# Hybrid attention-retention layer, one core: attention's q and k produced by features instead of by tokens; which third of the projection the first stage computes

## The chip, the cores and the metric

One NeuronCore of a Trainium2 chip runs the whole layer, 256 tokens by 1,024 features, in one launch. The metric is device time in microseconds. The kernel before was timed three times: 421.24, 421.24 and 421.31 us, median 421.24. All arithmetic is float32, and most matrix products are made from float32 operands split into a rounded high part and a remainder ("hi" and "lo"), with three products per pair: high by high, high by low, low by high.

## The reference, cut to what matters

```python
def token_mixer(h, w_in, w_proj_moba, w_proj_ret, w_out):
    proj = h @ w_in              # 256 x 1024 @ 1024 x 6656
    mq, mk, mv, rq, rk, rv, rg, g_a, g_r = split(proj)   # 512,512,512,512,512,1024,1024,1024,1024
    mq = rotary_half(split_heads(mq, 8), pos)   # 8 heads of 64: x1*cos - x2*sin, x2*cos + x1*sin
    mk = rotary_half(split_heads(mk, 8), pos)   # x1, x2: first and second 32 features of a head
    y_a = moba_attention(mq, mk, split_heads(mv, 8))     # 256 tokens: one block, plain causal attention
    rq = retnet_rotate(split_heads(rq, 4), pos)          # 4 heads of 128, features in even/odd pairs
    rk = retnet_rotate(split_heads(rk, 4), pos) * 128 ** -0.5
    y_r = head_norm(retention(rq, rk, split_heads(rv, 4)))   # decayed q k^T v, then mean 0, variance 1 per head
    y_r = silu(rg) * y_r
    merged = sigmoid(g_a) * (y_a @ w_proj_moba) + sigmoid(g_r) * (y_r @ w_proj_ret)
    return merged @ w_out
# around it: h = x * (1 + sc1) + sh1 with sc, sh from silu(c) @ w_ada; two layer norms; a gated FFN of width 2816
```

## The kernel before, in words

**First stage (0 to 63 us of the profiled execution).** The modulation vectors come from rows of `w_ada` by vector sums ("ada" work); as each of the eight 128-feature slices of the modulated input `h` is ready, it is multiplied with 2,048 columns of `w_in` (and the first four slices with those of g_a): all eight PSUM banks `pa[0..7]` collect mq and mk (1,024 columns, banks 0 to 3), mv (512, banks 4 and 5) and the first half of rv (512, banks 6 and 7), for both token halves. So q, k, v and rv arrive with tokens on the partitions.

**Main stage.** Everything else is a list of weight *units* of 1 MB (128 x 2,048). A unit is two halves and is worked off in two *steps* on PE. The list starts: four `wrot` units (rq and rk, units 0 to 3), six `winB` units (second half of rv, both halves of rg), two `winGa`, four `winGr`, two `wpm`, four `wpr`, and so on. Every half is prepared ahead: ScalarE (ACT) rounds it into `whi`, VectorE (DVE) subtracts to get `wlo` (`prep_halves`, eight buffers of each). There are two shapes of unit. `merged` (lines 134 and 138) keeps the weights stationary and gives results by features: 16 matmuls of 512 columns and 16 of 256. `xstat` (lines 123 to 125) keeps the input stationary and gives results by tokens: 24 matmuls of 512 columns.

**Side work.** `mixers` (attention) and `retention` are Python generators. `run_sides` advances them three times per step, and what they issue lands in the queues of PE, DVE and ACT between the pieces of the main list; nothing reorders it later, so each engine executes exactly the written order. Attention before: `evac_A` adds the two partial sums of q and k into `qk`; `rope` rotates them by tokens on DVE (lines 1020 to 1024, one call per token half), `rot_T` transposes both on PE (16 transposes, line 1030) into `qkT`; `scores` (line 1084) multiplies q by k for four heads per call, with 64 rows per head, so that two heads share the array; `maxima` (line 1093) masks and takes row maxima on DVE; ACT takes exponentials (line 1119) with sums; DVE the reciprocals (line 1123); ACT scales (line 1115); PE transposes the probabilities (line 1130); `attend` (line 1106) multiplies with v.

Retention's rq and rk come from `wrot` units, by features, one feature of each pair in one tile and its partner in another; `copied` moves the main and the correction part out of PSUM (line 499), `rotate` (lines 1001 to 1009) adds them and rotates on DVE. Scores (line 1190) and values (lines 1178 to 1180) follow on PE; mean and variance per head come from `bn_stats` and `bn_aggr` on DVE (lines 1170, 1171).

**Queues.** SP issues the weight loads in list order, each when one of four `raw` buffers is free; POOL issues the loads of `decay`, `x` and the norm rows. The constant tables are loaded on SP after the second unit (`CONST_AT`). Some of the later `ada` rows are mixed into the same stream (`extra`): two vector sums of 1,024 columns (line 257) per unit of theirs, placed after the preparation of a main half.

Of the kernel before, what the change touches and what calls it, by code (L numbers as in the profile page):

```python
# [19 lines left out]
RROPE, RET_AT, TL = 2, 10, 4  # L20
# [4 lines left out]
ROT_AT, RV_AT, RG_AT, LN1_AT = 4, 12, 20, 48  # L25
# [43 lines left out]
def _body(nc, a, out, pe, act, dve, sp, cst, wts, big, tmp, ps, dram):  # L69
# [267 lines left out]
    qk = [slot(n, [128, 1024]) for n in ("2a", "2b")]  # L337
# [151 lines left out]
    S = {}  # L489
    ghh, ghl = (lambda k: hh[:, k]), (lambda k: hl[:, k])  # L490

    S["rot"] = [slot(f"R{n}", [128, 4, 256]) for n in range(2)]
    S["rotl"] = [slot(n, [128, 4, 256]) for n in ("7a", "7b")]

    def wstat_rot(n, w):

        def copied(half, p):
            for i, o in enumerate((S["rot"][n], S["rotl"][n])):
                act.activation(o[:, 2 * w + half], p[:, i * 256:(i + 1) * 256], AF.Copy)
# [6 lines left out]
    def rv_done(bk):  # L506
        for t in range(2):
            act.activation(S["rv"][t][:, 512:], bk[t], AF.Copy)

    xstat("winB", 0, ghh, ghl, 8, lazy(two_banks), rv_done)  # L510
    for cc in range(2):
        def rg_done(bk, cc=cc):
            if cc == 0:
                S["rg"] = [slot(n, [128, 1024]) for n in ("7a", "7b")]
            for t in range(2):
                o = S["rg"][t][:, cc * 512:(cc + 1) * 512]
                act.activation(o, bk[t], AF.Silu)
        xstat("winB", 2 + 2 * cc, ghh, ghl, 8, lazy(two_banks), rg_done)
# [477 lines left out]
    def rotate(n):  # L996

        x, tmp_ = S["rot"][n], slot("8a", [128, 4, 256])
        xv, tv = (t.rearrange("p (w a) t -> p w a t", a=2) for t in (x, tmp_))
# [3 lines left out]
        for i in range(2):
            dve.tensor_tensor(tv[:, :, i], xv[:, :, 1 - i], bc(consts["sinr"], 2), OP.mult)
        yield
        dve.tensor_tensor(x, x, bc(consts["cosr"], 4), OP.mult)
        yield
# [3 lines left out]
    def rope(x, cos, sin):  # L1011

        n, w = cos.shape[-1], x.shape[-1]
        heads = w // n
        t2 = slot("8a", [128, w])
        hv = lambda t: t.rearrange("p (h n) -> p h n", n=n)
        bc = lambda v, m: v.unsqueeze(1).to_broadcast([128, heads, m])
        h2 = n // 2
        for i in range(2):
            dve.tensor_tensor(hv(t2)[:, :, i * h2:(i + 1) * h2],  # L1020
                              hv(x)[:, :, (1 - i) * h2:(2 - i) * h2],
                              bc(sin[:, i * h2:(i + 1) * h2], h2), OP.mult)
        dve.tensor_tensor(hv(x), hv(x), bc(cos, n), OP.mult)
        dve.tensor_tensor(x, x, t2, OP.add)

    def rot_T(roped, t, dst, which, b):

        p = bank(b)
        for i in range(4):
            pe.transpose(p[:, i * 128:(i + 1) * 128],  # L1030
# [453 lines left out]
```

## Time and profile before

| | |
|---|---|
| median of three runs | 421.24 us |
| profiled execution, its own time | 421.02 us |
| its span, first to last instruction | 419.3 us |
| PE busy | 413.1 us, 2,108 matmuls |
| DVE busy | 371.3 us |
| ACT busy | 246.7 us |
| granted TensorE clock | 0.997 |
| HBM traffic | 251 GB/s over the span |

The span is shorter than the time of its own run by 1.7 us, which lies before the first and after the last instruction. A matmul's listed duration overlaps that of the next one, so what a matmul costs in a stream is read from the distance between starts, not from its duration.

### The profile page before, as it was taken

How to read it: one execution, taken by the hardware profiler on the slowest of the kernel's cores; microseconds unless marked ns; L12 is line 12 of the kernel's file. 1: busy time of each engine (PE TensorE's matmuls, PEld its weight loads, DVE VectorE, ACT ScalarE, POOL GpSimd, SP SyncE). 2: the span in 40 equal slices, each digit the busy share in tenths (PEclk: the TensorE clock that was granted, in tenths of full speed). 3: DMA queues.
4: the chain of work that ended last, by engine and by line, in shares of the span. 5: the costliest groups of instructions: out<-in, count | busy, mean ns of one | idle time of the engine just before them, and what ended most of it. 6: DMA issues, size and time to landing. Idle time of an engine off the chain costs nothing.

```text
span 419.3 us, 5814 instructions
## 1 busy us (share of the span) xinstructions
PE 413.1 (99%) x2108; PEld 347.2 (83%) x2108; DVE 371.3 (89%) x605; ACT 246.7 (59%) x410; POOL 14.0 (3%) x26
## 2 busy tenths in 40 slices
PE   8999999999999999999999999999999999999995
PEld 4888888888878888888888898888888888888884
DVE  5979899969998889799787889899999998789996
ACT  4666568787855588535544886363563555455700
POOL 0000000100001000001000000100000000003200
PEclk9999999999999999999999999999999999999998
DMA  8998997685688778779672083995776877550002
GB/s 296 406 409 340 410 412 292 245 332 203 220 305 316 270 244 342 310 302 341 232 277 102 1 302 120 321 379 196 303 272 223 311 282 267 193 195 0 2 4 97
DMA packets 18540, 105.58 MB, mean 252 GB/s; under 512 B 2256, under 2 KB 3536, under 8 KB 7760
## 3 DMA queue, kind: packets, MB, share of 16 engines
q1 hardware_dynamic: 16992, 99.70, 63.0%
q0 software_dynamic: 1376, 4.99, 3.5%
q10 hardware_dynamic: 144, 0.52, 0.4%
q8 instruction: 16, 0.26, 0.3%
q14 instruction: 12, 0.10, 0.1%
HBM read 104.15 MB, written 1.06 MB: 251 GB/s over the span
## 4 chain that ended last, share of the span: by engine, by line
PE 98%; DVE 1%; issue 0%; DVEq 0%; ACT 0%; ACTq 0%
PE P L134 21%; PE P L123 14%; PE P L125 14%; PE P L124 14%; PE P L331 13%; PE P L138 11%; PE P L717 1%; PE P L720 1%; PE P L719 1%; PE P L1084 1%; PE P L243 1%; PE P L1190 1%; PE P L1106 1%; PE P L1130 1%; PE P L222 0%; PE P L661 0%
## 5 line engine op out<-in xcount | busy, mean ns | idle before, releaser
L1311 DVE TENSOR_TENSOR wlo<-raw,whi 128x1024 fp32r<-128x1024 f32 x118 | 141.6, 1219 | 11.6 <-ACT whi L1297 11.5
L1297 ACT ACTIVATE whi<-raw 128x1024 fp32r<-128x1024 f32 x118 | 121.7, 1056 | 33.9 <-PE P L125 10.8
L123 PE MATMUL P<-whi,AH 128*128 128x512 f32 x128 | 50.6, 395 | 0.0
L125 PE MATMUL P<-whi,AH 128*128 128x512 f32 x128 | 49.9, 390 | 0.0
L124 PE MATMUL P<-wlo,AH 128*128 128x512 f32 x128 | 49.8, 389 | 0.0
L134 PE MATMUL P<-AYa,whi 128*128 128x512 f32 x160 | 46.3, 391 | 0.0
L134 PE MATMUL P<-AYb,whi 128*128 128x512 f32 x160 | 43.0, 390 | 0.0
L331 PE MATMUL P<-whi,AH 128*128 128x512 f32 x160 | 41.6, 390 | 0.1
L257 DVE CUSTOM_DVE_ANT_0 junk<-raw,srow 128x1024 bf16<-128x1024 f32 x32 | 39.0, 1218 | 0.0
L331 PEld LDWEIGHTS P<-whi,AH 128*128 128x128 f32 x160 | 30.0, 188 | 7.1 <-ACT whi L314 0.9
L134 PEld LDWEIGHTS P<-AYb,whi 128*128 128x128 f32 x160 | 30.0, 188 | 6.6
L134 PEld LDWEIGHTS P<-AYa,whi 128*128 128x128 f32 x160 | 28.8, 189 | 4.7
L475 ACT ACTIVATE A<-P 128x256 f32<-128x256 f32 x40 | 15.0, 376 | 29.0 <-PE P L138 14.5
L314 ACT ACTIVATE whi<-raw 128x512 fp32r<-128x512 f32 (+1 forms) x26 | 20.8, 823 | 17.4 <-DMA raw<-in_b 16.1
L317 DVE TENSOR_TENSOR wlo<-raw,whi 128x512 fp32r<-128x512 f32 (+1 forms) x26 | 23.6, 935 | 6.0 <-ACT whi L314 5.5
L123 PEld LDWEIGHTS P<-whi,AH 128*128 128x128 f32 x128 | 24.0, 188 | 5.2 <-issue 0.3
L125 PEld LDWEIGHTS P<-whi,AH 128*128 128x128 f32 x128 | 24.0, 188 | 5.0
L124 PEld LDWEIGHTS P<-wlo,AH 128*128 128x128 f32 x128 | 24.0, 188 | 4.8
L138 PE MATMUL P<-AYb,wlo 128*128 128x256 f32 x160 | 25.7, 283 | 0.0
L138 PE MATMUL P<-AYa,wlo 128*128 128x256 f32 x160 | 25.6, 283 | 0.0
L138 PEld LDWEIGHTS P<-AYa,wlo 128*128 128x128 f32 x160 | 23.3, 190 | 1.6
L331 PE MATMUL P<-wlo,AH 128*128 128x512 f32 x80 | 23.2, 390 | 0.0
(308 smaller groups left out, 736.2 us busy)
## 6 DMA issues: line engine op xcount, KB each, us to landing
raw<-in_ada SPq DMA_DIRECT2D x16, 1024.0 KB, 4.9
raw<-in_wup SPq DMA_DIRECT2D x11, 1024.0 KB, 5.3
raw<-in_wgate SPq DMA_DIRECT2D x11, 1024.0 KB, 4.9
raw<-in_wdown SPq DMA_DIRECT2D x11, 1024.0 KB, 4.9
raw<-in_winB SPq DMA_DIRECT2D x6, 1024.0 KB, 5.4
raw<-in_m SPq DMA_DIRECT2D x4, 1024.0 KB, 8.1
raw<-in_b SPq DMA_DIRECT2D x4, 1024.0 KB, 7.3
raw<-in_wrot SPq DMA_DIRECT2D x4, 1024.0 KB, 7.9
```

Of the source, the lines that this page charges most:

```text
L123: pe.matmul(o, lh, rh, start=start, stop=False)
L124: pe.matmul(o, lh, rl, start=False, stop=False)
L125: pe.matmul(o, ll, rh, start=False, stop=stop)
L134: pe.matmul(banks()[half], t[0][:, k * 128:(k + 1) * 128], x2(k), start=k == 0, stop=half > 0 and k == 7)
L138: pe.matmul(banks()[half][:, :256], t[1][:, k * 128:(k + 1) * 128], x2(k)[:, 0], start=False, stop=half == 0 and k == 7)
L257: dve.tensor_tensor_reduce(out=nobody(j if own else None), in0=raw, in1=srow, scale=1.0, scalar=0.0, op0=OP.mult, op1=OP.add, accum_out=mo ...
L314: act.activation(hi[:, o], raw[:, o], AF.Copy)
L317: dve.tensor_tensor(lo[:, o], raw[:, o], f(hi[:, o]), OP.subtract)
L331: pe.matmul(pa[b0 + c // 512 * 2 + t], x[xi][:, j, t * 128:(t + 1) * 128], ws[k][:, c:c + 512], start=first and (xi, k) == (0, 0), stop=la ...
L475: act.activation(t, p[:, 256:], AF.Copy)
L1297: act.activation(hi, src, AF.Copy)
L1311: dve.tensor_tensor(lo, src, f(hi), OP.subtract)
```

## The change

- The first stage computes all of rv (1,024 columns, banks 0 to 3, kept in `S["rv"]`), mv as before, and the first half of rg (banks 6 and 7, through Silu on the way out of PSUM) instead of mq, mk, mv and half of rv.
- mq and mk become four more `wrot` units ahead of those of rq and rk: eight `wrot` units (steps 0 to 15), then two `winB` units (second half of rg). Tile `S["rot"][n]` for n = 0, 1 holds four heads of q and k: partitions 32e to 32e + 31 hold half of head e, the first and the second 32 features in separate slices. The total of units is the same.
- `rope` and `rot_T` are gone. `rotate` serves all four tiles, in two portions, put off to one and two steps after its second unit's last half.
- `scores` for four heads: for each head and query block two matmuls with 32 rows each, accumulated; the four heads sit on four row groups. It runs at the end of step 6 (heads 0 to 3) and of step 10 (heads 4 to 7), both times into banks 4, 7, 5, 6.
- The first two heads' probabilities are transposed one round later, into banks 4 and 7 (before: 5 and 6).
- Retention starts one step later. Its mean comes from the accumulating copies out of PSUM and its variance from eight Square activations on ACT instead of `bn_stats` and `bn_aggr` on DVE.
- cos and sin tables of both kinds are by features now: one extra load of 512 KB (`angles`) right after a smaller `tables` (180 KB; before 564 KB).
- The Sigmoid of `ga` is one activation per pair, put off by one or two steps.

```diff
-RROPE, RET_AT, TL = 2, 10, 4
+RET_AT, TL = 11, 4
-ROT_AT, RV_AT, RG_AT, LN1_AT = 4, 12, 20, 48
+SCORES_AT, RV_AT, RG_AT, LN1_AT = 6, 12, 20, 48
...
+        v = slot("8b", [128, 4, 256])
+        sp.dma_start(v, a["angles"])
+        for i, name in enumerate(ANGLES):
+            consts[name] = v[:, i]
...
-    S["rot"] = [slot(f"R{n}", [128, 4, 256]) for n in range(2)]
-    S["rotl"] = [slot(n, [128, 4, 256]) for n in ("7a", "7b")]
+    S["rot"] = [slot(n, [128, 4, 256]) for n in ("3a", "3b", "R0", "R1")]
+    S["rotl"] = [slot(n, [128, 4, 256]) for n in ("5", "15")] * 2
...
+            if w == half == 1:
+                turn = rotate(n)
+                put_off(1, lambda: next(turn))
+                put_off(2, lambda: next(turn))
         merged(a["wrot"][2 * n + w], lambda k: h1x2[:, :, k], copied)
-    for n in range(2):
+    for n in range(4):
         for w in range(2):
             wstat_rot(n, w)
...
     def rotate(n):
+        cos, sin = [consts[e + "mmrr"[n]] for e in ("cos", "sin")]
...
         dve.tensor_tensor(x, x, S["rotl"][n], OP.add)
+        for i in range(2):
+            dve.tensor_tensor(tv[:, :, i], xv[:, :, 1 - i], bc(sin, 2), OP.mult)
         yield
...
+        dve.tensor_tensor(x, x, bc(cos, 4), OP.mult)
         for i, op in enumerate((OP.subtract, OP.add)):
             dve.tensor_tensor(xv[:, :, i], xv[:, :, i], tv[:, :, i], op)
...
-        S["rv"] = [slot(n, [128, 1024]) for n in ("6a", "6b")]
+        S["rg"] = [slot(n, [128, 1024]) for n in ("7a", "7b")]
         for t in range(2):
-            act.activation(S["rv"][t][:, :512], pa[6 + t], AF.Copy)
+            act.activation(S["rg"][t][:, :512], pa[6 + t], AF.Silu)
...
-            S["sc"] = [bank(b) for b in ((4, 7, 5, 6), (2, 3, 4, 7))[h // 4]]
-            for w in range(2):
-                for qb, c in enumerate(blk):
-                    for e in range(2):
-                        s = slice(64 * e, 64 * e + 64)
-                        pe.matmul(S["sc"][2 * w + e][:, c], qkT[0][s, h // 2 + w, qb * 128:(qb + 1) * 128],
-                                  qkT[1][s, h // 2 + w, :128 + 128 * qb], start=True, stop=True)
+            S["sc"] = [bank(b) for b in (4, 7, 5, 6)]
+            x = S["rot"][h // 4]
+            for qb, c in enumerate(blk):
+                for i in range(2):
+                    for e in range(4):
+                        s = slice(32 * e, 32 * e + 32)
+                        pe.matmul(S["sc"][e][:, c], x[s, i, qb * 128:(qb + 1) * 128], x[s, 2 + i, :128 + 128 * qb],
+                                  start=i == 0, stop=i == 1)
...
-            for h in {4: (0, 1), 8: (2, 3, 4, 5), 10: (6, 7)}.get(i, ()):
+            for h in {5: (0, 1), 8: (2, 3, 4, 5), 10: (6, 7)}.get(i, ()):
                 sm, mx = st.pop(h)
-                p = bank(h - 2 if h in (2, 3) else 5 + h % 2)
+                p = bank((4, 7, 4, 7, 5, 6, 5, 6)[h])
...
-                    dve.bn_stats(stt[:, 2 * g + t % 2], yr[t % 2][:, g * 256:(g + 1) * 256])
-                    dve.bn_aggr(mv[:, 2 * g + t % 2], stt[:, 2 * g + t % 2:2 * g + t % 2 + 1])
+                    e = 2 * g + t % 2
+                    act.activation(square, yr[t % 2][:, g * 256:(g + 1) * 256], AF.Square, bias=mv[:, 1, e:e + 1],
+                                   accum_out=mv[:, 2, e:e + 1])
...
-        wrot=np.stack([ws(wi[:, RQ + 512 * w:][:, half_pairs(n)], 0, 2) for n in range(2) for w in range(2)]),
-        winB=np.stack(sum([xs(wi, RV + 512 * i) for i in range(1, 4)], [])),
+        wrot=np.stack([ws(wi[:, 512 * w:][:, half_heads(n)], 0, 2) for n in range(2) for w in range(2)] +
+                      [ws(wi[:, RQ + 512 * w:][:, half_pairs(n)], 0, 2) for n in range(2) for w in range(2)]),
+        winB=np.stack(xs(wi, RG + 512)),
```

How instructions stand now. The numbers behind names tell one buffer's uses apart and are not the same in both programs.

**ACT at the seam of the two stages.** `P4` to `P7` are the banks of mv and of rv (before) or rg (now); `whi` are the rounded weight halves of the main stage. Before:

```order
L1297 ACTIVATE whi_618<-raw_594 128x1024
L1045 ACTIVATE A4_624<-P4_130 128x512
L1045 ACTIVATE A4_624<-P5_131 128x512
L1048 ACTIVATE AYa_83<-P6_132 128x512
L1048 ACTIVATE AYb_84<-P7_133 128x512
L1297 ACTIVATE whi_634<-raw_594 128x1024
L1297 ACTIVATE whi_638<-raw_596 128x1024
L1297 ACTIVATE whi_644<-raw_596 128x1024
L499 ACTIVATE AR0_584<-P0_648 128x256
```

Now:

```order
L1260 ACTIVATE whi_620<-raw_596 128x1024
L1020 ACTIVATE A4_626<-P4_130 128x512
L1020 ACTIVATE A4_626<-P5_131 128x512
L1023 ACT_TABLE_LOAD
L1023 ACTIVATE A7a_629<-P6_132 128x512
L1023 ACTIVATE A7b_630<-P7_133 128x512
L1260 ACTIVATE whi_633<-raw_596 128x1024
L1260 ACTIVATE whi_637<-raw_598 128x1024
L1260 ACTIVATE whi_643<-raw_598 128x1024
L502 ACTIVATE AYa_83<-P0_647 128x256
```

The two copies of rv have become two Silu of rg, with a table load ahead of them, and the weight halves 5, 6 and 7 stand behind it.

**DVE in steps 0 to 6.** `A2a`, `A2b` are q and k by tokens, `AYa` the first tile of q and k by features, `A5` its correction part. Before:

```order
L1311 TENSOR_TENSOR wlo_616<-raw_590,whi_608 128x1024
L1311 TENSOR_TENSOR wlo_620<-raw_590,whi_614 128x1024
L1020 TENSOR_TENSOR A8a_629<-A2a_134,tables_592 128x16x32 x2
L1023 TENSOR_TENSOR A2a_134<-A2a_134,tables_592 128x1024
L1024 TENSOR_TENSOR A2a_134<-A2a_134,A8a_629 128x1024
L1311 TENSOR_TENSOR wlo_636<-raw_594,whi_618 128x1024
L1311 TENSOR_TENSOR wlo_640<-raw_594,whi_634 128x1024
L1311 TENSOR_TENSOR wlo_646<-raw_596,whi_638 128x1024
L1020 TENSOR_TENSOR A8a_669<-A2b_135,tables_592 128x16x32 x2
L1023 TENSOR_TENSOR A2b_135<-A2b_135,tables_592 128x1024
L1024 TENSOR_TENSOR A2b_135<-A2b_135,A8a_669 128x1024
L1311 TENSOR_TENSOR wlo_693<-raw_596,whi_644 128x1024
```

Now (the first row is half 6; `wlo_741` is half 10):

```order
L1274 TENSOR_TENSOR wlo_645<-raw_598,whi_637 128x1024
L1274 TENSOR_TENSOR wlo_687<-raw_598,whi_643 128x1024
L1274 TENSOR_TENSOR wlo_693<-raw_614,whi_685 128x1024
L1274 TENSOR_TENSOR wlo_735<-raw_614,whi_691 128x1024
L1274 TENSOR_TENSOR wlo_741<-raw_624,whi_733 128x1024
L1002 TENSOR_TENSOR AYa_83<-AYa_83,A5_586 128x1024
L1004 TENSOR_TENSOR A8a_743<-AYa_83,A8b_594 128x2x256 x2
L1006 TENSOR_TENSOR AYa_83<-AYa_83,A8b_594 128x1024
L1008 TENSOR_TENSOR AYa_83<-AYa_83,A8a_743 128x2x256 x2
L1274 TENSOR_TENSOR wlo_792<-raw_641,whi_739 128x1024
L1274 TENSOR_TENSOR wlo_798<-raw_641,whi_790 128x1024
```

The two rotations by tokens, each between weight halves early in the stage, are gone; one rotation by features stands behind half 10.

**DVE between the first and the second group of scores.** `mx` are row maxima of a head, `junk` rows are the `ada` sums. Before, behind the maxima of heads 2 and 3:

```order
L1001 TENSOR_TENSOR AR0_584<-AR0_584,A7a_586 128x1024
L1311 TENSOR_TENSOR wlo_924<-raw_743,whi_887 128x1024
L257 ISA junk_926,mod_82<-raw_695,srow_100 128x1024
L257 ISA mod_82 128x1
L1123 RECIPROCAL mx_914<-mx_914 128x2
L1004 TENSOR_TENSOR A8a_920<-AR0_584,tables_592 128x2x256 x2
L1311 TENSOR_TENSOR wlo_951<-raw_743,whi_922 128x1024
L257 ISA junk_955,mod_82<-raw_821,srow_100 128x1024
L257 ISA mod_82 128x1
L1123 RECIPROCAL mx_917<-mx_917 128x2
L1093 ISA A11_848,mx_998<-P2_986,tables_592 128x128
```

Now, from the same place:

```order
L1006 TENSOR_TENSOR AYb_84<-AYb_84,A8b_594 128x1024
L1008 TENSOR_TENSOR AYb_84<-AYb_84,A8a_888 128x2x256 x2
L1086 RECIPROCAL mx_914<-mx_914 128x2
L1274 TENSOR_TENSOR wlo_947<-raw_737,whi_876 128x1024
L261 ISA junk_951,mod_82<-raw_794,srow_100 128x1024
L261 ISA mod_82 128x1
L1274 TENSOR_TENSOR wlo_955<-raw_872,whi_945 128x1024
L261 ISA junk_957,mod_82<-raw_794,srow_100 128x1024
L261 ISA mod_82 128x1
L1086 RECIPROCAL mx_917<-mx_917 128x2
L1055 ISA A11_821,mx_1007<-P4_987,tables_592 128x128
```

Where a quarter of retention's rotation stood, which PE reads only at line 1190, stands now the second half of the rotation of `AYb`, the q and k of heads 4 to 7, which line 1046 (their scores) reads next. Its first half stands ahead of the maxima of heads 2 and 3, behind two weight halves and two `ada` sums that follow the first reciprocal. The maxima of head 4 in the last row read bank 4, which is also the bank of head 0's transposes.

More of the change, by code (lines that the diff above doesn't have):

```diff
@@ L335, in g_prod @@
         x_prod(f"g{j}", ks, j == 0, j == 3)
-    qk = [slot(n, [128, 1024]) for n in ("2a", "2b")]
+    S["rv"] = [slot(n, [128, 1024]) for n in ("2a", "2b")]
     ga = slot(12, [128, 4, 512])
@@ L499, in copied, with rg_done @@
                 act.activation(o[:, 2 * w + half], p[:, i * 256:(i + 1) * 256], AF.Copy)
+            if w == half == 1:
+                turn = rotate(n)
+                put_off(1, lambda: next(turn))
+                put_off(2, lambda: next(turn))
         merged(a["wrot"][2 * n + w], lambda k: h1x2[:, :, k], copied)
-    for n in range(2):
+    for n in range(4):
         for w in range(2):
             wstat_rot(n, w)
-    def rv_done(bk):
+    def rg_done(bk):
         for t in range(2):
[L508 to L518, printed above, removed]
+            act.activation(S["rg"][t][:, 512:], bk[t], AF.Silu)
+    xstat("winB", 0, ghh, ghl, 8, lazy(two_banks), rg_done)
     for c in range(2):
@@ L1001, in rotate @@
         dve.tensor_tensor(x, x, S["rotl"][n], OP.add)
+        for i in range(2):
+            dve.tensor_tensor(tv[:, :, i], xv[:, :, 1 - i], bc(sin, 2), OP.mult)
         yield
[L1003 to L1007, printed above, removed]
+        dve.tensor_tensor(x, x, bc(cos, 4), OP.mult)
         for i, op in enumerate((OP.subtract, OP.add)):
             dve.tensor_tensor(xv[:, :, i], xv[:, :, i], tv[:, :, i], op)
[L1011 to L1030, printed above, removed]
-                         roped[:, which * 512 + i * 128:which * 512 + (i + 1) * 128], ident)
-        act.activation(dst[which][:, :, t * 128:(t + 1) * 128],
-                       p.rearrange("p (i t) -> p i t", i=4), AF.Copy)
+        yield
     def evac_A():
@@ L1107, in attend @@
                                   v[:, kb, 64 * u:64 * u + 64], pT[e][:, c], start=kb == 0, stop=kb == 1)
-            return lambda: split(yah[:, h // 2:h // 2 + 2], yal[:, h // 2:h // 2 + 2], p.rearrange("p (w t) -> p w t", w=2))
-        for i in range(HM + 5):
+            return lambda: split(S["yah"][:, h // 2:h // 2 + 2], S["yal"][:, h // 2:h // 2 + 2],
+                                 p.rearrange("p (w t) -> p w t", w=2))
+        for i in range(HM + 6):
             yield
@@ L1139, in mixers @@
                 maxima(i + i % 2)
-            if i == RROPE:
-                S["turn"] = [rotate(n) for n in range(2)]
-            if i >= RROPE and S["turn"] and next(S["turn"][0], 1) == 1:
-                S["turn"].pop(0)
             if i == RET_AT:
@@ L1150, in retention @@
     def retention():
-        rot, decay, sms = S["rot"], S["decay"], S["sms"]
+        rot, decay, sms = S["rot"][2:], S["decay"], S["sms"]
         while S["main"] < RV_AT:
@@ L1156, in retention @@
         rv = S["rv"]
-        yr = [slot(n, [128, 1024]) for n in ("8a", "8b")]
-        SCORES, VALUES = ((4, 7), (2, 3)), (5, 6, 4, 7)
-        stt = tmp.tile([128, 8, 6], F32, name="stt", bufs=1)
-        mv = tmp.tile([128, 8, 2], F32, name="mvr", bufs=1)
+        SCORES, VALUES = ((4, 7), (0, 1)), (5, 6, 4, 7)
+        mv = tmp.tile([128, 3, 8], F32, name="mvr", bufs=1)
+        square = decay[0][:, 0, :256]
         sd = tmp.tile([128, 8], F32, name="sdr", bufs=1)
@@ L1216, in retention @@
                 for t in range(2):
[L1217 to L1218 removed]
+                    dve.scalar_tensor_tensor(yr[t][:, c], yr[t][:, c], mv[:, 1, 2 * g + t:2 * g + t + 1], srg[t][:, c],
+                                             op0=OP.add, op1=OP.mult)
             yield
@@ L1225, in retention @@
             yield
-        for _ in range(11):
+        for _ in range(8):
             yield
@@ L1471 @@
     ins.update(_tables())
+    ins["angles"] = np.stack([ins.pop(n) for n in ANGLES], 1)
     ins["tables"] = np.concatenate([np.asarray(ins.pop(n), dtype=np.float32).reshape(128, -1) for n, _ in TABLES], 1)
```

55 lines of the change are left out of this document (22 added, 33 removed).

## The prediction

> **What bounds the kernel now.** I read the page's busy times and its chain first, then the windows by stage, then the timelines of PE, ACT and DVE between 62 and 102 us, where the change moves work.
>
> ```profile
> span 419.3 us, 5814 instructions
> PE 413.1 (99%) x2108; PEld 347.2 (83%) x2108; DVE 371.3 (89%) x605; ACT 246.7 (59%) x410; POOL 14.0 (3%) x26
> PE 98%; DVE 1%; issue 0%; DVEq 0%; ACT 0%; ACTq 0%
> ```
>
> The third line is the chain that ended last: 98% of the span lies on PE. So a microsecond of PE work added or removed is a microsecond of time, and so is a microsecond in which PE waits. DVE is at 89%, so the second question is whether DVE can still deliver on time. The windows (time, then busy time of each engine) say where:
>
> ```profile
> 62.98:84.53 21.55, 21.55 (x130) 19.05 (x128) 21.14 (x21) 17.13 (x31) 1.27 (x2) 1.00 0.75 272
> 84.53:101.99 17.46, 17.46 (x102) 14.29 (x102) 13.69 (x42) 14.49 (x39) 0.00 (x0) 1.00 0.72 270
> 101.99:128.73 26.74, 26.74 (x167) 21.98 (x165) 25.04 (x44) 18.93 (x42) 0.00 (x0) 1.00 0.73 272
> 128.73:172.00 43.27, 43.27 (x194) 36.09 (x193) 39.52 (x68) 28.66 (x44) 1.06 (x2) 1.00 0.81 290
> ```
>
> PE has no gap in any of them. The third busy column is DVE: 21.1 of 21.6, 13.7 of 17.5, 25.0 of 26.7. From the start of the main stage to retention DVE has almost no room.
>
> **PE's own work.** PE's timeline (start, duration of the run, line, count; the distance between starts is the cost):
>
> ```profile
> 62.98 2.20 PE L134 MATMUL P<-AH,whi 128*128 128x512 f32 x9
> 66.94 3.82 PE L134 MATMUL P<-AH,whi 128*128 128x512 f32 x16
> 72.50 3.82 PE L134 MATMUL P<-AH,whi 128*128 128x512 f32 x16
> 79.69 1.03 PE L1030 MATMUL P<-ident,A2a 128*128 128x128 f32 x8
> 80.56 1.04 PE L1030 MATMUL P<-ident,A2b 128*128 128x128 f32 x8
> 81.35 2.30 PE L134 MATMUL P<-AH,whi 128*128 128x512 f32 x9
> 84.53 1.58 PE L1084 MATMUL P<-AYb,AYa 64*128 64x128 f32 x16
> 86.04 1.22 PE L138 MATMUL P<-AH,wlo 128*128 128x256 f32 x8
> 88.72 0.39 PE L123 MATMUL P<-whi,AH 128*128 128x512 f32 x1
> 96.88 0.82 PE L1130 MATMUL P<-ident,A 128*128 128x128 f32 x6
> 97.63 1.58 PE L1084 MATMUL P<-AYb,AYa 64*128 64x128 f32 x16
> 99.14 0.50 PE L123 MATMUL P<-whi,AH 128*128 128x512 f32 x1
> ```
>
> *Four units change shape.* A `merged` unit takes 72.50 - 66.94 = 5.56 us. Between 88.72 and 96.88 stand three `xstat` steps of 12 matmuls: 8.16 / 36 = 0.227 us each, 5.44 us a unit of 24. Four units cost 4 x 0.12 = +0.48 us.
>
> *Sixteen transposes go:* 81.35 - 79.69 = -1.66 us.
>
> *Scores.* One call takes 86.04 - 84.53 = 1.51 us (99.14 - 97.63 gives the same), for 16 matmul records on two row groups of 64. The new call has 32 records of the same widths on four row groups of 32, an arrangement that this trace does not show. If four run at once as two do now, the call stays at 1.51; if only two do, it is 3.02. I take 1.51, since the row is one of row groups that do run side by side, and keep 3.02 as the other end. The sum for the two calls is 0 to +3.0.
>
> In sentences of their own: the Trainium skill, "TensorE: Matmul & The Clock Gate", Part 3 on packing small matmuls, gives 3.07 times the speed for four row tiles of 32, not four times. By that a call would be an estimated 1.51 x 4 / 3.07 = 2.0 us; it speaks against the case of only two at a time, and this trace, with two groups only, can't show it.
>
> So without any new wait PE gains 1.66 - 0.48 = **1.2 us**. That is what the change is worth if DVE and ACT are never late.
>
> **When q and k are ready now.** Before, `rope` ran from the first step on, and PE's transposes came at 79.69 with time to spare. Now the rotation can start only when units 0 and 1 are through PE (62.98 + 2 x 5.56 = 74.1), and it stands behind half 10 in DVE's queue. When half 10 comes is set by ACT, whose timeline before is:
>
> ```profile
> 65.94 1.07 ACT L1045 ACTIVATE A<-P 128x512 f32<-128x512 f32 x2
> 66.90 0.60 ACT L1048 ACTIVATE AYa<-P 128x512 f32<-128x512 f32 x1
> 67.37 0.61 ACT L1048 ACTIVATE AYb<-P 128x512 f32<-128x512 f32 x1
> 67.85 2.97 ACT L1297 ACTIVATE whi<-raw 128x1024 fp32r<-128x1024 f32 x3
> 70.70 0.40 ACT L499 ACTIVATE AR<-P 128x256 f32<-128x256 f32 x1
> 71.75 2.06 ACT L1297 ACTIVATE whi<-raw 128x1024 fp32r<-128x1024 f32 x2
> 85.31 1.28 ACT L1119 ACT_TABLE_LOAD   x1
> 86.61 0.40 ACT L1119 ACTIVATE A<-A,mx 128x128 f32<-128x128 f32 x1
> 87.41 0.19 ACT L1119 ACTIVATION_READ_ACCUMULATOR A<-A,mx 128x1 f32 x1
> ```
>
> Three halves take 70.70 - 67.85 = 2.85 us, 0.95 each, and four copies of a step pair 71.75 - 70.70 = 1.05. The table load for Silu is new at this place: 1.28 us by the row of the one for Exp. The old order from 66.90, with the load: load to 68.2; two Silu as the two copies, 0.95, to 69.15; halves 5 to 7, to 72.0; copies of unit 0, to 73.05; halves 8 and 9, to 74.95; copies of unit 1, whose results are there since 74.1, to 76.0; half 10, whose last element is there at 77.1. ACT has no pause in this stretch.
>
> DVE, where the times of the operations come from the same operations before:
>
> ```profile
> 66.59 1.29 DVE L1020 TENSOR_TENSOR A8a<-A2a,tables 128x512 f32<-128x512 f32 x2
> 67.91 1.22 DVE L1023 TENSOR_TENSOR A2a<-A2a,tables 128x1024 f32<-128x1024 f32 x1
> 69.17 1.22 DVE L1024 TENSOR_TENSOR A2a<-A2a,A8a 128x1024 f32<-128x1024 f32 x1
> 70.31 3.49 DVE L1311 TENSOR_TENSOR wlo<-raw,whi 128x1024 fp32r<-128x1024 f32 x3
> 85.49 0.29 DVE L1093 CUSTOM_DVE_ANT_0 A<-P,tables 128x128 f32<-128x128 f32 x1 [0.78 <-PE P L1084]
> 86.05 0.28 DVE L1093 CUSTOM_DVE_ANT_0 A<-P,tables 128x128 f32<-128x128 f32 x1
> 86.61 0.08 DVE L1093 DVE_READ_ACCUMULATOR2_ANT mx<- 128x1 f32 x1
> 87.63 0.17 DVE L1123 RECIPROCAL mx<-mx 128x2 f32<-128x2 f32 x1 [0.94 <-ACT A L1119]
> 87.72 1.21 DVE L1311 TENSOR_TENSOR wlo<-raw,whi 128x1024 fp32r<-128x1024 f32 x1
> 88.84 1.22 DVE L257 CUSTOM_DVE_ANT_0 junk<-raw,srow 128x1024 bf16<-128x1024 f32 x1
> 89.98 0.09 DVE L257 DVE_READ_ACCUMULATOR2_ANT mod<- 128x1 f32 x1
> ```
>
> A pair of 512 takes 1.32 from start to start when the next operation needs it, a 1,024-wide one 1.26; one that needs nothing follows 1.14 after. A weight half or an `ada` sum takes 1.14, the maxima of a head 86.05 - 85.49 = 0.56. A rotation is two wide operations and two pairs: 1.26 + 1.32 + 1.26 + 1.2 = 5.0 us.
>
> *First scores.* Half 10's remainder 77.1 to 78.3, rotation to **83.3**. PE, without transposes, reaches the scores after 3 units and the stretch that took 84.53 - 81.35 = 3.18: 62.98 + 16.68 + 3.18 = **82.84**. PE waits about 0.4 us: scores from 83.2 to 84.75.
>
> *Second scores.* DVE goes on from 83.3: two halves (85.6), maxima of heads 0 and 1 (86.7), then the reciprocal, which waits for ACT's exponential of head 0. Head 0's maxima are there at 86.15, and the exponential of a head takes from 86.61 to 87.6, 1.0: 87.15. Then half, `ada`, half, `ada` (4.6: 91.8), the first half of the rotation of heads 4 to 7 (2.5: 94.3), the maxima of heads 2 and 3 (1.1: 95.4), the second half (2.5): **97.9**. PE from 84.75: rest of step 6 and step 7, 88.72 - 86.04 = 2.68; one unit, 5.56; step 10, 3.18: **96.2**. PE waits 1.7 us, less the quarter of the scores that needs only the first half of the tile (0.2): 1.5. The scores end at about 99.2.
>
> *First transposes.* PE does step 11 (2.68) and is at 101.9 at the transposes of heads 0 and 1, now in banks 4 and 7, which heads 4 and 5 have just filled. DVE empties them after half, `ada`, half, `ada` (4.6) and 0.56: 97.9 + 4.7 + 0.56 = **103.2**, and 103.75 for bank 7. PE waits 1.3 and 0.2 us. Before, these transposes used banks 5 and 6, long empty.
>
> Together PE waits 0.4 + 1.5 + 1.5 = **3.4 us**. All three waits lie on one chain of DVE work from 77.1 to 103.7 with one pause of 0.4. So the cost of the scores on PE hardly enters: a slower call takes the place of a wait.
>
> **After that.** Where DVE takes retention's scores, it had time before:
>
> ```profile
> 127.52 1.02 DVE L1193 TENSOR_TENSOR A<-P,A2a 128x384 f32<-128x384 f32 x2 [1.48 <-PE P L1190]
> ```
>
> It was there at 126.04 and waited 1.48 us for PE. Behind 104 us it has one rotation, one half and one `ada` sum more than before ahead of this place; adding the rows in the new order it is there at 132.0, 6.0 later. PE comes 2.4 us later by the sum below and has one step (12 x 0.227 = 2.7) more, 5.1 later. So DVE's pause shrinks to about 0.6, and no wait of PE arises. Weight halves are four or more ahead of PE at all three waits above, so none of them becomes a wait either. From 128.73 on, DVE loses `bn_stats` and `bn_aggr`, and ACT gets eight Squares with sums, some 0.6 us each by the exponential's rows: 28.7 + 5 of 43.3 us. Both are taken as free; if Squares stood in the way of a weight half, they would cost up to these 5 us, but the halves are ahead. The constant loads (692 against 564 KB, an estimated 0.5 us at the window's 272 GB/s) lie ahead of unit 2's weights on SP's queue; ACT rounds the second half of unit 2 at 67.85 before and at 69.15 now, and it is the Silu that it waits for. They cost 0.
>
> **The sum.** -1.66 + 0.48 + 0 (scores) + 3.4 = **+2.2 us**, and about 0.1 us for the stream that restarts after a wait (0.50 against 0.39 us in the rows at 99.14 and 88.72): +2.4 in round numbers. Against the profiled execution's own 421.02 us that is 423.4. This execution lies 0.22 us under the median, so I predict **423.6 us**.
>
> **Rivals.**
>
> *DVE keeps up.* Then only PE's work counts: 421.24 - 1.2 = 420.0 us, faster. The place is half 10. If it did not stand behind ACT's Silu and copies, the rotation could start at 75.1, when ACT has copied unit 1 out (74.1 + 1.05), and be done at 80.1, 3.2 us earlier, and the whole chain with it; nearly all of the waits would go. For it: a wait for several events may end earlier than I take it to. Against it: ACT's rows add up without a pause. It decides from 3 us of gain on; every us less than that leaves one us more of waiting: 1.5 us of gain gives 421.9, inside no change.
>
> *Only two row groups at a time.* Scores take 3.02. The first call then ends at 86.2, DVE's maxima start 0.9 us later than above, the second rotation ends at 98.8, the second call at 101.5; after step 11 PE is at 104.2, and bank 4 is ready by then. The transposes end 0.9 us later than in the forecast: 424.5 us.
>
> *A fourth wait, in retention.* DVE's pause at the decay products is only 0.6 us. If the chain between 104 and 132 us is 3 us longer, by exponentials that come late for the reciprocals between its halves, the products and with them the value matmuls come some 2 us late: 425.6 us. It decides from 0.6 us of delay on. Against it: this stretch has the same kinds of rows as before, in which DVE arrived early.
>
> **How the numbers follow.** Chances: waits as computed, within a microsecond, 0.50; two row groups 0.12; fourth wait 0.10; DVE partly early (between 420.4 and 422) 0.12; DVE keeps up 0.16. A measurement of this kernel can tell about 0.2% (0.84 us) from no change. Faster by more than that is the last case alone, 0.16; no change 0.13 with the edges of its neighbours; slower 0.71. The likeliest case by itself spans 422.6 to 424.6. The range takes in the slower cases and most of the partly early one: **420.3 to 425.6**.
>
> **What would show it.** In the new PE timeline: no line 1030, a gap ahead of the scores at line 1046 of about 0.4 and 1.5 us and one ahead of the first transposes at line 1094, all released by DVE; DVE nearly without a pause from half 10 to the maxima of head 4. Scores of 1.5 us show four row groups side by side, of 3 us two. No Silu load between the first stage's copies, or half 10 on DVE before 75 us, would make the first step wrong, and PE without gaps there the whole forecast.

## The result, and the profile after

The changed kernel takes **425.85 us** (median of 4 runs, 425.27 to 426.35) against 421.27 us for the kernel before beside it (4 runs): ratio 1.0108, 95% interval 1.0090 to 1.0125. It is slower, as forecast, but by 4.6 us where 2.4 were computed; 425.85 lies 0.25 us above the range. The profiled execution took 426.35 us, the longest of its four. All ratios here and below are of runs at a granted clock of 0.989 or more; a single run of 591.64 us at 0.657, of the kernel with blocks 8 and 15 below, is left out of them.

The page of the changed kernel (span; busy times and counts; the chain that ended last):

```profile
span 424.6 us, 5936 instructions
PE 413.3 (97%) x2156; PEld 347.1 (82%) x2156; DVE 370.6 (87%) x593; ACT 252.3 (59%) x441; POOL 14.0 (3%) x26
PE 87%; DVE 6%; ACT 3%; DMA 2%; issue 1%; DVEq 0%; ACTq 0%
```

PE is busy for 413.3 us, as before (413.1). The chain, 98% PE before, is now 87% PE: the rest passed to DVE, ACT and the transfers. So PE does no more work than before (a part of the 413.3 us is even pauses inside rows, see below); it waits. The view of waits, for PE (what it waited for, total, times, longest):

```profile
PE P L134 <- ACT A L502: 1.4, 1, 1.4
PE P L1046 <- DVE AYa L1008: 1.3, 1, 1.3
PE P L1094 <- DVE mx L1055: 1.2, 1, 1.2
PE P L1046 <- DVE AYb L1008: 1.1, 1, 1.1
```

None of the four is there before; together 5.0 us. PE's timeline puts them in place:

```profile
75.76 2.35 PE L134 MATMUL P<-AH,whi 128*128 128x512 f32 x9 [1.38 <-ACT A L502]
85.94 1.97 PE L1046 MATMUL P<-AYa 32*128 32x128 f32 x32 [1.33 <-DVE AYa L1008]
87.85 1.22 PE L138 MATMUL P<-AH,wlo 128*128 128x256 f32 x8
100.29 1.97 PE L1046 MATMUL P<-AYb 32*128 32x128 f32 x32 [1.06 <-DVE AYb L1008]
102.20 1.22 PE L138 MATMUL P<-AH,wlo 128*128 128x256 f32 x8
106.23 1.07 PE L1094 MATMUL P<-ident,A 128*128 128x128 f32 x6 [1.20 <-DVE mx L1055]
```

The last three stand where the prediction put its waits. The first, inside unit 2, is new: the next matmul of unit 2 needs a bank from which ACT has not yet copied unit 0. A scores call takes 87.85 - 85.94 = 1.91 us, which looks like a slower array, but is not; see the experiments.

Why is ACT late? Its rows in the changed kernel:

```profile
67.90 1.06 ACT L1260 ACTIVATE whi<-raw 128x1024 fp32r<-128x1024 f32 x1 [3.27 <-DMA raw<-in_wrot]
69.94 1.28 ACT L1023 ACT_TABLE_LOAD   x1
79.05 2.08 ACT L1260 ACTIVATE whi<-raw 128x1024 fp32r<-128x1024 f32 x2
```

and the same weight half (half 4, the first of unit 2) before:

```profile
64.98 1.06 ACT L1297 ACTIVATE whi<-raw 128x1024 fp32r<-128x1024 f32 x1 [1.91 <-PE P L134]
```

Before, ACT took half 4 at 64.98; now it takes it at 67.90, 2.9 us later, and waited for the **transfer** of the weights. The row of before names PE as what ended the wait, but the view of DMA issues shows that there too the transfer came last (KB, us from issue to landing, of unit 2's load; before, then after):

```profile
raw<-in_wrot SPq DMA_DIRECT2D x1, 1024.0 KB, 8.8
raw<-in_wrot SPq DMA_DIRECT2D x1, 1024.0 KB, 11.2
```

Issued at 56.04 us, the load landed at 64.84 before; issued at 56.60, it lands at 67.8 now. So 0.6 of the 2.9 us are a later issue (in this execution SP is already 0.6 us later at 48.3 us, ahead of every load that the change moved), and 2.4 us are a longer transfer. The table load (1.28) and everything behind it are as computed, only some 3 us later: half 10 is taken at 79.05, computed was 76.0.

What delays the transfer? The issues on SP and POOL, before:

```profile
53.79 0.42 SPq L163 DMA_DIRECT2D tables<-in_tables  x1
56.04 3.87 SPq L110 DMA_DIRECT2D raw<-in_wrot  x2
81.04 0.72 POOL L1072 DMA_DIRECT2D A2a<-in_decay  x1 [79.67 <-DVE wlo L1311]
```

and after:

```profile
53.49 0.72 POOL L1033 DMA_DIRECT2D AYa<-in_decay  x1 [52.11 <-ACT A7a L306]
58.21 0.54 POOL L1033 DMA_DIRECT2D AYb<-in_decay  x1 [4.00 <-ACT A7b L306]
54.83 0.47 SPq L189 DMA_DIRECT2D A8b<-in_angles  x1
56.60 18.28 SPq L110 DMA_DIRECT2D raw<-in_wrot  x5
```

The two loads of retention's decay table (384 KB each, from the tile's 128 x 2 x 384 float32) have moved from 81 to 53 and 58 us. Nobody wrote them there: they now go into tiles 6a and 6b instead of 2a and 2b, those tiles are free early, and POOL issues a load as soon as its tile is free. With the new `angles` load on SP, 1.25 MB stand in the stretch in which the weights of units 2 and 3 arrive. The windows of that stretch (the last three columns are clock, busy share of the transfer engines and GB/s), before:

```profile
66.00:68.00 2.00, 2.00 (x15) 1.82 (x14) 1.97 (x4) 2.00 (x6) 0.00 (x0) 1.00 0.88 340
```

and after:

```profile
66.00:68.00 2.00, 2.00 (x15) 1.82 (x15) 1.49 (x2) 0.10 (x1) 0.00 (x0) 1.00 1.03 426
```

Before, the transfers had room here and ACT (fourth busy column) was busy for all 2.00 us. After, they are full at 426 GB/s and ACT does 0.10 us of work.

DVE continues from there. Its rows after (half 10; start of the first rotation; end of the second; maxima of head 4; decay products):

```profile
80.22 1.22 DVE L1274 TENSOR_TENSOR wlo<-raw,whi 128x1024 fp32r<-128x1024 f32 x1 [0.62 <-ACT whi L1260]
81.36 1.22 DVE L1002 TENSOR_TENSOR AYa<-AYa,A 128x1024 f32<-128x1024 f32 x1
99.55 1.29 DVE L1008 TENSOR_TENSOR AYb<-AYb,A8a 128x512 f32<-128x512 f32 x2
105.46 0.27 DVE L1055 CUSTOM_DVE_ANT_0 A<-P,tables 128x128 f32<-128x128 f32 x1
135.66 1.02 DVE L1156 TENSOR_TENSOR A<-P,AYa 128x384 f32<-128x384 f32 x2 [0.85 <-PE P L1153]
```

Half 10's remainder starts 3.1 us later than computed (80.22 for 77.1), the second rotation ends 2.9 us later (100.8 for 97.9). The length of the chain was right, its start was not. At the decay products DVE still waits 0.85 us for PE: no fourth wait arose.

### The profile page after: what moved, and what is told of

It reads as the page before. It is cut to its first block, busy times and chain, and to the rows that moved or that the text cites. A ratio compares the mean times of both kernels' runs of the same rounds, so it can differ in the third digit from the quotient of the medians.

```text
span 424.6 us, 5936 instructions
## 1 busy us (share of the span) xinstructions
PE 413.3 (97%) x2156; PEld 347.1 (82%) x2156; DVE 370.6 (87%) x593; ACT 252.3 (59%) x441; POOL 14.0 (3%) x26
## 3 DMA queue, kind: packets, MB, share of 16 engines
HBM read 104.28 MB, written 1.06 MB: 248 GB/s over the span
## 4 chain that ended last, share of the span: by engine, by line
PE 87%; DVE 6%; ACT 3%; DMA 2%; issue 1%; DVEq 0%; ACTq 0%
PE P L134 20%; PE P L123 12%; PE P L125 12%; PE P L124 12%; PE P L335 11%; PE P L138 10%; DVE wlo L1274 2%; DMA raw<-in_b 2%; ACT whi L1260 1%; DVE junk L261 1%; PE P L717 1%; PE P L719 1%; PE P L720 1%; PE P L1153 1%; PE P L1068 1%
## 5 line engine op out<-in xcount | busy, mean ns | idle before, releaser
L335 PE MATMUL P<-whi,AH 128*128 128x512 f32 x160 | 41.9, 391 | 0.1
L123 PE MATMUL P<-whi,AH 128*128 128x512 f32 x96 | 37.9, 395 | 0.0
L125 PE MATMUL P<-whi,AH 128*128 128x512 f32 x96 | 37.4, 390 | 0.0
L124 PE MATMUL P<-wlo,AH 128*128 128x512 f32 x96 | 37.4, 389 | 0.0
L335 PEld LDWEIGHTS P<-whi,AH 128*128 128x128 f32 x160 | 29.8, 188 | 7.5 <-ACT whi L318 0.8
L134 PE MATMUL P<-AH,whi 128*128 128x512 f32 x128 | 31.3, 393 | 1.4 <-ACT A L502 1.4
L134 PEld LDWEIGHTS P<-AH,whi 128*128 128x128 f32 x128 | 23.4, 188 | 6.3 <-ACT A L502 1.8
L335 PE MATMUL P<-wlo,AH 128*128 128x512 f32 x80 | 23.2, 390 | 0.0
L806 DVE SCALAR_TENSOR_TENSOR A<-A,tables 128x255 f32<-128x255 f32 (+1 forms) x44 | 21.3, 484 | 1.6
```

The source lines that it names most:

```text
L123: pe.matmul(o, lh, rh, start=start, stop=False)
L124: pe.matmul(o, lh, rl, start=False, stop=False)
L125: pe.matmul(o, ll, rh, start=False, stop=stop)
L134: pe.matmul(banks()[half], t[0][:, k * 128:(k + 1) * 128], x2(k), start=k == 0, stop=half > 0 and k == 7)
L335: pe.matmul(pa[b0 + c // 512 * 2 + t], x[xi][:, j, t * 128:(t + 1) * 128], ws[k][:, c:c + 512], start=first and (xi, k) == (0, 0), stop=la ...
L806: dve.scalar_tensor_tensor(g[:, 2 - n:], x[:, :254 + n], w(n), g[:, 2 - n:], op0=OP.mult, op1=OP.add)
```

## The experiments

**Which load delays unit 2?** The first three kernels put the loads to a later place, one at a time and together.

*Decay late.* A write of one element per partition to each tile, on DVE in the step of the first scores, holds POOL's load back until then.

```diff
+            dve.memset(S["decay"][i][:, 0, :1], 0.0)
             nc.gpsimd.dma_start(S["decay"][i], a["decay"][i])
```

> The changed kernel, with one element of each decay tile set on VectorE in step 6 right before its load, so that POOL's two decay loads (768 KB) start at about 86 us instead of 53.5 and 58.2. Theory (the early decay loads hold up the weights of unit 2, by about 2 us, and the chain from ScalarE's half 4 over VectorE to the first transposes moves one for one): half 4 is rounded at about 65.5 instead of 67.9, the first rotation ends near 84, no wait of TensorE at unit 2, about 423.9 us. Rival (the 512 KB of angles, put ahead of unit 2 on SP's queue, are what is late): half 4 stays near 67.5 and the time near 425.6. Rival (neither: the computed chain was simply too short): no change, 425.8.

Measured: 423.98 us, ratio to before 1.0065 (1.0050 to 1.0080). That is 1.9 us less than the changed kernel. ACT takes half 4 at 65.43 instead of 67.90.

*Angles late.* The `angles` load moves from behind `tables` to behind the weights of unit 3 on SP's queue. All of it moves, 512 KB, though the change added only 128 KB to the constants in sum (692 for 564 KB); so this is not a pure undoing.

> The changed kernel, with the load of the angles put behind the weights of unit 3 on SP's queue; the decay loads stay early. Theory (decay): SP's queue is now lighter by 384 KB ahead of unit 2 than in the kernel before, the decay loads cost about 2 us: half 4 at about 66.5, time about 424.6 us. Rival (angles): half 4 at 65.0 and 423.5 us. Rival (neither): 425.8.

Measured: 423.98 us, ratio 1.0075 (1.0057 to 1.0094). Also 1.9 us less, which falls between the two theories' numbers; ACT takes half 4 at 65.57.

*Both late.*

> Both at once: decay loads gated to step 6 and angles behind unit 3. Theory: unit 2's weights arrive as in the kernel before or earlier, half 4 is rounded at 65.0, no wait at unit 2, and the chain is the predicted one: waits of about 0.4, 1.5 and 1.5 us, 423.5 us. If the chain had a second cause of lateness of its own, the time stays above 424.

Measured: 422.96 us (422.81 to 423.44), ratio 1.0044 (1.0029 to 1.0059): 2.9 us less than the changed kernel, less than the sum of the two, since ACT now has half 4 early enough (PE's wait for the first rotation is gone):

```profile
63.60 1.06 ACT L1263 ACTIVATE whi<-raw 128x1024 fp32r<-128x1024 f32 x1 [0.97 <-DMA raw<-in_wrot]
```

Half 4 is 1.4 us earlier here than in the kernel before (63.60 for 64.98), since all of the angles have gone from ahead of it; the next kernel shows that a still earlier chain on ACT gains nothing. So the early loads cost 2.9 of the 4.6 us, and 1.8 us against the kernel before beside it (421.12) remain: the part that the prediction had computed at 2.4. The waits of PE in this run, and from the timeline its scores calls with DVE's last two operations of the second rotation:

```profile
PE P L1097 <- DVE mx L1058: 1.2, 1, 1.2
PE P L1049 <- DVE AYb L1010: 1.0, 1, 1.0
```

```profile
82.89 1.59 PE L1049 MATMUL P<-AYa 32*128 32x128 f32 x32
84.42 1.22 PE L138 MATMUL P<-AH,wlo 128*128 128x256 f32 x8
96.10 1.29 DVE L1010 TENSOR_TENSOR AYb<-AYb,A8a 128x512 f32<-128x512 f32 x2
96.84 1.97 PE L1049 MATMUL P<-AYb 32*128 32x128 f32 x32 [1.04 <-DVE AYb L1010]
98.75 1.22 PE L138 MATMUL P<-AH,wlo 128*128 128x256 f32 x8
```

The first call, which waits for nothing, takes 84.42 - 82.89 = **1.53 us**; the second, which waits, 1.91. PE starts as soon as the first of the rotation's last two operations is done (half of the pair's 96.10 to 97.39, so some 96.75) and pauses within the call for the second; the waits view counts only the pause ahead of the first matmul, and 0.38 us hide in the row's duration. Four row groups of 32 do run side by side: twice the matmuls in the time of the 16 on two groups (1.51). The Trainium skill ("TensorE: Matmul & The Clock Gate", Part 3, the measured speedups) gives 3.07 for four row tiles with 512 columns, which would have been an estimated 2.0 us a call; with the 128 and 256 columns here this trace does not agree, its 1.53 is what four times gives. The estimate and the four times both count two row groups as twice as fast as one, which no run here measures.

**Is it Silu's table load that makes the first half late?** Added to both loads late: the first half of rg is only copied out of PSUM at the seam, and Silu follows in place in step 17, where the second half's Silu runs anyway.

```diff
-            act.activation(S["rg"][t][:, :512], pa[6 + t], AF.Silu)
+            act.activation(S["rg"][t][:, :512], pa[6 + t], AF.Copy)
```

> As the run with both loads late, and the half of rg from the first stage is only copied at the seam; its Silu is done in place with that of the other half in step 17. ScalarE loses a table load of 1.28 us ahead of half 5. Theory (one chain from ScalarE's half 5 to VectorE's maxima of head 4): every wait behind it starts 1.3 us earlier, 422.2 us. Rival (the waits come from VectorE's own amount of work between the scores, wherever the chain begins): 423.3 us, as without this edit.

Measured: 423.00 us, ratio 1.0042 (1.0026 to 1.0059): no gain. The table load is gone, but behind it ACT waits for PE:

```profile
74.63 0.38 ACT L504 ACTIVATE AYa<-P 128x256 f32<-128x256 f32 x1 [0.64 <-PE P L134]
```

These are the copies of unit 1, which stand ahead of half 10. So half 10 hangs on PE's own unit 1, not on the table load, and the rival's number holds. Its reason, that what DVE has to do between the two scores calls sets the remaining waits, is put to the test next.

**Is it?** Between the first scores and the maxima of heads 4 and 5, DVE makes four modulation (`ada`) sums, which nobody needs before the second norm. They stand behind weight blocks 6 and 7 of the stream, by a table of places. The next three kernels move those two blocks behind 15 and 17:

```diff
-    for sec, at in ((2, (6, 7, 9, 10)), ...
+    for sec, at in ((2, (9, 10, 15, 17)), ...
```

> Both loads late, and two of the four modulation blocks of section 2 move in the weight stream from behind weight blocks 6 and 7 to behind blocks 15 and 17, which takes four VectorE sums (4 x 1.22 us and their read-outs, 5.2 us) out of the stretch between the first scores and the maxima of heads 4 and 5. Theory (what VectorE has to do between the two scores calls sets the two remaining waits): the second rotation ends 2.5 us earlier, at 94.9 us, where TensorE is done with what stands ahead at 95.8, and the maxima of heads 4 and 5 end 5 us earlier than TensorE needs them; the waits of 1.04 and 1.21 us and a pause of 0.4 inside the second scores call vanish, 422.96 - 2.65 = 420.3 us (419.9 to 420.8), under the 421.1 of the kernel before. Rival (VectorE is short over the whole stretch from 80 to 160 us, so that the waits reappear where the sums now stand): 422.0 to 423.0 us, with a new wait of TensorE for VectorE after 140 us.

Measured: 423.07 us, ratio 1.0051 (1.0039 to 1.0064): no gain in time. But PE's waits no longer list the theory's two (lines 1049 and 1097); a new one has come at 181.7 us:

```profile
PE P L123 <- DVE A L542: 2.4, 1, 2.4
```

```profile
177.01 1.06 ACT L1263 ACTIVATE whi<-raw 128x1024 fp32r<-128x1024 f32 x1 [3.75 <-DMA raw<-in_wpr]
```

The rival had the place and the price, but not the reason: it is not DVE that is short there. The moved blocks stand in the same four load buffers, ahead of the `wpr` weights; ACT waits 3.75 us for those, its copies and DVE's products come late behind it, and PE finds its bank full.

> The changed kernel as it is, its two loads early, with only the four sums moved. Theory: the late start stays (TensorE waits 1.4 us for ScalarE's copies out of the bank and 1.3 us for the first rotation), the later waits go (1.06 and 1.20 us and 0.4 us inside the second scores call): 425.85 - 2.65 = 423.2 us (422.8 to 423.7). Rival (one cause behind all four waits, the late start alone): the chain is 2.9 us late from the start on, so without the sums it catches up only by part, 424.5 to 425.5 us.

Measured: 426.11 us (424.84 to 427.42), ratio 1.0123 (1.0101 to 1.0145). Again the two later waits are gone and the first two (1.4 and 1.3) stay, as the theory says; PE takes retention's scores at 131.65 us instead of 134.05. Again the wait at `wpr` (1.6 us) takes most of the gain, and the runs spread by 2.6 us.

> The kernel before, with only the four sums moved. Theory: TensorE waits for VectorE nowhere in this stretch of the kernel before, so that the time stays: 421.1 us (420.7 to 421.5). Rival (the sums where they stand cost the kernel before as well, so that a gain in the first of these runs would not be the changed kernel's own): 419.5 to 420.3 us.

Measured: 428.01 us, ratio 1.0163 (1.0147 to 1.0178). Neither number: the kernel before gets the wait at `wpr` too, 4.6 us long there (to 187.12 us), and the granted clock is 0.50 from 186 to 192 us. The twelve matmuls from 187.12 to 192.38 us take 5.26 us instead of 2.72, so that wait and clock together cost 7.2 us. Ahead of it nothing is gained: PE takes retention's scores at 126.13 us (before 125.91, with a main stage that starts 0.2 us earlier). So this place is bad for any of the kernels, and says nothing against the theory.

**Better places.** Both loads late, and other places for the two blocks.

> Both loads late, modulation blocks of section 2 behind weight blocks 8, 9, 10 and 21 instead of 6, 7, 9 and 10: two sums (2.5 us) now between 104 and 112 us, two near 198 to 206 us, where VectorE had 2.9 us of 8 free and the four weight blocks asked for together at 186 us keep the transfers busy. Theory (the two waits between the scores go with the sums, the wait of 2.4 us at 181.7 us came from ScalarE's weight blocks, which stood behind the moved modulation blocks in the four load buffers between 150 and 180 us): no wait before 190 us, 422.96 - 2.25 = 420.7 us (420.2 to 421.2). Rival (any later place delays the weights behind it by as much): 422 to 423.5 us, with a new wait of TensorE after 104 us.

> Both loads late, the two modulation blocks behind weight blocks 21 and 22. Theory: as with 8 and 21, no wait before 190 us, 420.7 us (420.2 to 421.2), as long as the two blocks of 1 MB, some 2.6 us each at the 380 GB/s of that stretch, don't make the output projection's weights late. Rival: they do, and TensorE waits 1 to 4 us for ScalarE or for the weights between 200 and 222 us: 421.5 to 424.5 us.

> Both loads late, the two modulation blocks behind weight blocks 8 and 15. Theory: half of the delay that blocks 15 and 17 gave the weights of 160 to 180 us: the wait there falls from 2.4 to 0 to 1.2 us, 420.7 to 421.9 us. Rival (one block there is enough to make ScalarE's weight late by the whole 2.4 us): 423 us.

> Both loads late, only the block behind weight block 7 moves, to behind block 8: the two sums that VectorE made at 98.5 and 100.8 us, between the second rotation and the maxima of heads 4 and 5, are gone from there, the two at 87.2 and 90.1 us stay. Theory: the wait for the second rotation stays (1.04 us, and 0.4 inside the second scores call), the wait for the maxima (1.21 us) goes: 422.96 - 1.2 = 421.75 us (421.4 to 422.1). Rival (the sums count only together): 422.96 us.

| blocks of section 2 behind | us | ratio to before (95%) | PE's listed waits behind 63 us, without the last 0.4 |
|---|---|---|---|
| 8 and 21 | 421.50 | 1.0004 (0.9995 to 1.0013) | 0.3 at 199 us |
| 21 and 22 | 422.34 | 1.0031 (1.0021 to 1.0041) | 0.6 and 0.7 at 207 and 209 us |
| 8 and 15 | 421.01 | 1.0000 (0.9989 to 1.0011) | none |
| 6 and 8 | 422.21 | 1.0024 (1.0014 to 1.0033) | 1.0 ahead of the second scores |

With 8 and 15 the changed kernel takes the time of the kernel before. All of PE's waits in that run:

```profile
PE P L228 <- DVE srow L226: 1.6, 1, 1.6
PE P L337 <- DVE AH L303: 0.6, 1, 0.6
PE P L883 <- ACT AYb L881: 0.4, 1, 0.4
```

The first and the last are in every run, the second is in the first stage, ahead of anything changed. But the view does not list pauses inside a group of matmuls. The transposes of heads 6 and 7, with blocks 8 and 15 and, below it, with both loads late alone:

```profile
116.19 1.50 PE L1097 MATMUL P<-ident,A 128*128 128x128 f32 x6
118.90 0.82 PE L1097 MATMUL P<-ident,A 128*128 128x128 f32 x6
```

The first group starts 0.2 us late and lasts 0.7 us longer. Two sums behind block 8 now stand ahead of the DVE work that leads to these transposes, and ACT scales the last head's probabilities at 116.38 us; with 21 and 22, where no sum was moved there, it does so at 113.96, and the group takes 0.81. All three tables with block 8 have this row of 1.50. It fits that 8 and 21 (421.50, forecast 420.2 to 421.2) and 6 and 8 (422.21, forecast 421.4 to 422.1) end above their ranges; 8 and 15 lies within its own. With 6 and 8, where only the two sums behind the second rotation are gone, the wait for the maxima goes and that for the rotation stays, as the theory said. With 21 and 22 the rival holds in part: the waits are there, and 1.3 us long.

**Do the causes add, and is the move worth as much to the kernel before?** The same table, 8 and 15, in the changed kernel with its loads early, and in the kernel before:

> The changed kernel with its two loads early, only the modulation blocks behind 6 and 7 moved behind 8 and 15. Theory (two causes that add: the early loads' late start 2.9 us, the sums between the scores some 2 us): the waits of 1.06 and 1.20 us go, those of 1.4 and 1.3 us stay; 425.85 - 2.0 = 423.9 us (423.3 to 424.4). Rival (one chain, on which a gain at one place is lost at the next): 425 to 426 us.

> The kernel before, with the same two blocks behind 8 and 15. Theory: TensorE waits there for no sum, so nothing is to be gained: 421.2 us (420.8 to 421.6), or, if the block behind 15 makes the weights of 160 to 180 us late as the blocks behind 15 and 17 did (a wait of 4.6 us), up to 425. Rival (the moved sums are worth as much to the kernel before as to the changed one): 419.2 to 420.2 us.

The first took 423.67 us, ratio 1.0060 (1.0044 to 1.0076): 2.2 us less than the changed kernel, forecast 2.0. The two causes add. Of the two waits that were to stay, the one for the first rotation does (1.3); that in unit 2 is 0.3 us in the profiled execution, which has a wait of 1.0 us in the first stage instead. The second took 423.74 us, ratio 1.0074 (1.0048 to 1.0099), slower than the kernel before. There is nothing to be gained from the sums there: PE takes retention's scores at 125.85 us, before 125.91. And the block behind 15 makes the `wpr` weights late:

```profile
183.81 0.47 PE L123 MATMUL P<-whi,AYa 128*128 128x512 f32 x1 [1.63 <-ACT whi L1297]
```

So the sums are in the way of the changed kernel alone. Not tried: whether another table would make the kernel before faster.

## Why the prediction was right and wrong, point by point

- **PE's own work, -1.2 us.** Scores at 1.51 us a call: right, 1.53 where nothing waits. That a slower call "takes the place of a wait" was not put to the test. The 1.2 us show in the kernel with blocks 21 and 22, where PE waits for nothing up to retention: it takes retention's scores 64.73 us after the start of the main stage (62.81 to 127.54), the kernel before after 62.93 (62.98 to 125.91) and with one step less (2.72). A pause of 0.34 in the second scores call taken off, PE needs 1.26 us less: right. No table that was tried keeps this gain to the end: behind 21 and 22 waits at 207 us take it, with 8 and 15 the 0.9 us at 116 us and the pause in the second scores call.
- **"They cost 0."** This is the step that failed. It weighed the constants by their own duration (an estimated 0.5 us) and then found them covered by Silu. It did not list what else had moved in the queues: the decay loads on POOL are mentioned nowhere in the prediction, though the tile names in the change (2a, 2b to 6a, 6b) decide when POOL issues them. The runs put 2.9 us in its place, with a new wait of 1.4 us for ACT's copies and the first rotation 3.1 us late.
- **The ACT chain at the seam.** As a chain right (its rows follow each other as computed), but it was taken to begin at the old time and to be ACT's own. With both loads late half 10 is taken at 74.99 us, 1.0 earlier than computed, and the table load is covered, since ACT would wait for PE's unit 1 otherwise.
- **Wait 1, first scores, 0.4.** 1.33 us and 0.38 within the call in the changed kernel; none with both loads late. The term was too high for the chain as computed and too low for the chain as it came.
- **Wait 2, second scores, 1.5.** 1.06 + 0.38 = 1.4; with both loads late 1.04 + 0.38. Right, place and size. A late start does not lengthen it, since the first wait holds PE back by the same time.
- **Wait 3, first transposes, 1.5.** 1.20 and, with both loads late, 1.21, and a pause of 0.25 inside the group in both (six transposes take 106.23 to 107.06 in the changed kernel, 100.12 to 100.70 with blocks 8 and 15). Together 1.45: right, place and size. The pause fits the 0.2 that the prediction computed for the second bank.
- **"All three waits lie on one chain of DVE work."** Right: moving two sums out takes away the third wait alone, moving four takes away the second and third (each run above), and the time follows where no new wait or pause comes. The chain does not end there: with sums behind block 8 it reaches the transposes of heads 6 and 7.
- **After that, no wait in retention.** Right: a pause of 0.85 us, computed 0.6.
- **The sum.** Forecast +2.4. Listed waits of 4.97 us, two pauses of 0.38, one of 0.25 and PE's -1.2 make +4.8; measured is +4.6 on the medians, +5.3 on the profiled executions, from which the waits are. A listed wait begins at the modelled end of a matmul. From start to start, as the prediction counts, the four places lose 1.70 (unit 2), 1.78, 1.51 and 1.60 us; less 1.2 that is +5.4. With the loads out of the way the second and third wait, 1.49 and 1.61 in the same way, less 1.2 make +1.9; measured +1.8.
- **Rivals.** DVE keeping up and two row groups at a time are both excluded by the rows above, the fourth wait by DVE's pause. None of the cases was a late weight transfer, so the range of 425.6 ended short of it.

## What to carry to other kernels

When a change renames tiles, list every load into them: a load is issued when its tile is free, so a new tile moves the load, on whichever queue, and if it lands where the transfers are full, something else is late, here by about its transfer time. In a kernel whose queues run in written order, work that nobody waits for (here the modulation sums, 4.9 us by four rows of 1.22) may stand anywhere until a change puts a deadline behind it; then it is the first thing to move, but what it brings along (its load buffers) has to fit at the new place, which two of the five new tables missed with both loads late, and it must not come ahead of the next deadline, as it does behind block 8. Cost a chain of work from its true first input on, transfers included, not from its old start time.

## What was unexpected of the hardware

- Loads on POOL's queue delayed those on SP's as much as loads on SP's own. Unit 2's load takes 11.2 us from issue to landing in the changed kernel, 9.3 with the decay loads (768 KB) moved away, 9.8 with the angles (512 KB) moved away, 7.9 with both. That is 1.25 MB in 3.3 us, 397 GB/s; the stretch from 58 to 70 us ran at 395 to 426 GB/s.
- PE starts a group of matmuls when its first ones have their data, and a pause inside the group shows only in the row's length: 1.97 us against 1.59 for the same 32 matmuls.
- Late in PE's wait of 4.64 us, in the kernel before with blocks 15 and 17, the granted clock falls to 0.50 and stays there from 186 to 192 us, 5 us of them behind the wait; a matmul of 512 columns comes every 0.43 us instead of 0.23. In and behind waits of 2.42 and 1.63 us at the same place it is 1.00.
